# Sixteen of 64 rank pairs instead of sixteen of 256 in a product-key retrieval

## The chip, the cores and the metric

The kernel runs on one core of a Trainium2 chip, in one launch. The metric is the device time of that launch in microseconds (us). The engines are named as the profile names them: PE is TensorE (matmuls; PEld its weight loads), DVE is VectorE, ACT is ScalarE, POOL is GpSimd, and SP only issues DMAs here. Each engine takes its instructions from its own queue in order, and waits at the head of that queue for what the instruction needs.

## The reference

Two transformer blocks over 512 tokens of width 1024. The change concerns the feed-forward part of the first, a PEER layer: 16384 experts of one neuron each, found by product keys. For each token and each of 8 heads, two halves of a query are scored against 128 keys each, and the best 16 of each half are kept; the 256 sums of a first and a second score are searched for the best 16.

```
s_top, i_top = lax.top_k(s, PEER_TOPK)                     # (tokens, heads, 2, 16)
cand_s = (s_top[:, :, 0, :, None] + s_top[:, :, 1, None, :]).reshape(..., 256)
cand_i = (i_top[:, :, 0, :, None] * PEER_N_KEYS + i_top[:, :, 1, None, :]).reshape(..., 256)
best_s, best_pos = lax.top_k(cand_s, PEER_TOPK)
experts = jnp.take_along_axis(cand_i, best_pos, axis=-1)
g = jax.nn.softmax(best_s, axis=-1)
act = jax.nn.gelu(jnp.einsum('thkd,td->thk', expert_u[experts], xb))
return jnp.einsum('thk,thkd->td', g * act, expert_v[experts])
```

Since both lists of 16 are sorted, a pair of ranks (a, b), counted from 0, has at least (a+1)(b+1)-1 pairs before it, so that it can be among the first 16 only where (a+1)(b+1) is at most 16.

## The kernel before, in words

Every float32 matmul is done as three in a rounded float32 format: a weight tile `raw` of 128 x 1024 is loaded by SP (`weight`, line 857), ACT writes its rounded part `hi` (line 861), DVE the rest `lo = raw - hi` (line 863), and PE multiplies hi by the input's two parts and lo by the first (`mm3`, lines 867 to 869). `hi` and `lo` have three buffers each.

The PEER layer treats its 512 tokens in two ways. The fourth tile of 128 tokens gathers its experts' rows from memory (`gather`, line 164: per step an indirect DMA on POOL, a product with a sum on DVE, line 172, and an accumulation on DVE, line 169). The other 384 tokens are multiplied densely with all experts: 128 products of a weight tile `uT` with 384 tokens (`hidden`, line 372: 24 matmuls of 128 x 384 to a bank `ps_mm`, then a gelu on ACT). A product is called p0, p1, ... here in the order in which PE takes them. A dense matrix of gates, zero where an expert was not chosen, is built from one-hot matrices (`build`, line 182: `oh` and `gi` on DVE, `ps_S` on PE) and multiplied in before the second dense product (`output`, line 420).

The stages in order are: queries and first searches (lines 278 to 296, 16 times, over 128 scores each); retrieval beside the first products (lines 388 to 394); build beside further products (lines 400 to 406); the remaining products, each beside the output of the one before; and the outputs of those products that were kept in memory (`spill`).

`retrieve(n)` (line 298) is called for the four token tiles, n = 3 first. I call its four passes retrieval blocks. In each, for 8 heads, POOL adds the 256 sums (`cand`, line 306) and DVE searches them (`top16`, line 270: MAX8, MATCH_REPLACE8, MAX8, FIND_INDEX8 twice, the last three kinds preceded by a short load of the eight values). The places found, 0 to 255, are split in a first and a second rank by a shift and a mask (lines 315 and 317), and each rank is turned to a key index: DVE compares it with 0 to 15 (`eq`, line 321, 128 x 2048), POOL multiplies the 16 one-hot planes with the indices `tif` (line 323), and DVE adds the planes up by halves (lines 329 and 331). A softmax follows (lines 335 to 341), and for three of the tiles a transposition on PE (line 349).

What sets the order: the program interleaves the parts by credits (`Work.go`, line 211). A `yield 1.9` says that a step is worth 1.9 us; after each product, retrieval may use RH = 2.4 us of credit (line 391). From these, the number of products before the second stage follows, and from it the number of products kept in memory, which is rounded up to a multiple of IG = 8 (line 401). The framework's scheduler then gives every engine's queue its final order, by its own estimate of when an instruction's inputs are there.

Of the kernel before, what the change touches and what calls it, by code (L numbers as in the profile page):

```python
# [8 lines left out]
F32 = mybir.dt.float32  # L9
F32R = mybir.dt.float32r  # L10
BF16 = mybir.dt.bfloat16
I32 = mybir.dt.int32
U32 = mybir.dt.uint32
AF = mybir.ActivationFunctionType
ALU = mybir.AluOpType
# [3 lines left out]
P = 128  # L19
# [9 lines left out]
TOPK = 16  # L29
# [102 lines left out]
DT = 3  # L132
AB, LA = 3, 1
NR, TC, IG = 32, 24, 8
RH, GH0, BH, GH1, GF, GO, VP = 2.4, 1.0, 2.3, 1.2, 3.4, 4, 999


def peer(ctx, tc, I, banks, mod, mid, x1, R, vec, gain, ident, weight, mm3, proj, proj_many, split, enter):

    nc = tc.nc  # L140
    T = DT * P
    with ExitStack() as c2:
# [82 lines left out]
        with ExitStack() as c3:  # L225
# [3 lines left out]
            h = (hh, hl)  # L229
# [7 lines left out]
            with tc.tile_pool(name="tn", bufs=1) as tn:  # L237
# [6 lines left out]
                for c in HALVES:  # L244
                    for k in range(KB):
# [4 lines left out]
                                                       op0=ALU.add, op1=ALU.subtract)  # L250
# [6 lines left out]
            pq = c4.enter_context(tc.tile_pool(name="pq", bufs=1))  # L257
            tq = c4.enter_context(tc.tile_pool(name="tq", bufs=2))
# [2 lines left out]
            nc.vector.tensor_copy(iob, iof)  # L261
            ioa = pq.tile([P, TOPK, P], BF16, name="ioa")
            nc.vector.tensor_copy(ioa, iof[:, 0:TOPK, 0:1].broadcast_to([P, TOPK, P]))
            keysT = pq.tile([P, NHP, P], F32, name="keysT")
            nc.sync.dma_start(keysT, I["keysT"])

# [31 lines left out]
            def retrieve(n):  # L298
# [2 lines left out]
                tv = top[:, n].rearrange("p (h j) k -> p h j k", j=2)  # L301
                bs = tq.tile([P, 8, TOPK], F32, tag="bs", name="bs", bufs=1)
                bx = tq.tile([P, 8, TOPK], U32, tag="bx", name="bx", bufs=1)
                for hd in range(8):
                    cand = tq.tile([P, TOPK, TOPK], F32, tag="cand", name="cand", bufs=2)
                    nc.gpsimd.tensor_tensor(cand, tv[:, hd, 0, :].unsqueeze(2).broadcast_to([P, TOPK, TOPK]),
                                            tv[:, hd, 1, :].unsqueeze(1).broadcast_to([P, TOPK, TOPK]), ALU.add)
                    top16(cand.rearrange("p a b -> p (a b)"), bs[:, hd, :], bx[:, hd, :], 256)
                    yield 1.9
                ij = []  # L310
                for j in range(2):
                    pi = tq.tile([P, P], U32, tag="pi", name="pi", bufs=2)
                    flat = bx.rearrange("p h k -> p (h k)")
                    if j == 0:
                        nc.vector.tensor_scalar(pi, flat, 4, None, op0=ALU.logical_shift_right)
                    else:
                        nc.vector.tensor_scalar(pi, flat, 15, None, op0=ALU.bitwise_and)
                    pf = tq.tile([P, P], BF16, tag="pf", name="pf", bufs=2)
                    nc.vector.tensor_copy(pf, pi)
                    eq = tq.tile([P, TOPK, P], BF16, tag="eq", name="eq", bufs=2)  # L320
                    nc.vector.tensor_tensor(eq, pf.unsqueeze(1).broadcast_to([P, TOPK, P]), ioa, ALU.is_equal)
                    e4 = eq.rearrange("p a (h k) -> p h a k", h=8)
                    nc.gpsimd.tensor_tensor(e4, e4, tif[:, :, j, :].unsqueeze(3).broadcast_to([P, 8, TOPK, TOPK]), ALU.mult)
                    ij.append(eq)
                    yield 1.5
                for j in range(2):
                    eq = ij[j]
                    for w_ in (8, 4, 2):
                        nc.vector.tensor_add(eq[:, 0:w_], eq[:, 0:w_], eq[:, w_:2 * w_])
                    r = tq.tile([P, P], F32, tag="ij%d" % j, name="ij", bufs=1)  # L330
                    nc.vector.tensor_add(r, eq[:, 0], eq[:, 1])
                    ij[j] = r
                    yield 1.5
                ex = tq.tile([P, 8, TOPK], F32, tag="ex", name="ex", bufs=1)
# [978 lines left out]
```

## Time and profile before

| what | us |
|---|---|
| median of three runs (2555.66 to 2558.7) | 2557.21 |
| the profiled execution, its own time | 2557.7 |
| its span, first to last instruction | 2555.9 |
| PE busy in the span | 2476.8 |
| DVE busy in the span | 1787.7 |
| POOL busy in the span | 309.1 |

Busy time is the sum of an engine's instructions in the span; a matmul overlaps with its neighbours, so PE counts as busy also where its clock is low. The profile has the clock that was granted to TensorE beside each stretch: 1.00 is 2.4 GHz, 0.50 is 1.2 GHz. Its mean over this execution is 0.989. A view of waits says for each engine which instruction waited, for whom and how long; a timeline lists single instructions, and a bracket at a row's end says how long the engine had been idle before it, and for what.

### The profile page before, as it was taken

The page shows a single profiled execution, that of the slowest core. Times are in us where ns is not written, and L with a number is a line of the kernel's source. Part 1 is how long each engine was busy: PE and PEld are TensorE (multiplying, and loading weights), DVE is VectorE, ACT ScalarE, POOL GpSimd, SP SyncE. Part 2 cuts the span into 40 slices and gives each one's busy share as a digit, 9 for nine tenths or more (in the row PEclk, how much of TensorE's full clock was granted, in tenths as well). Part 3 has the DMA queues.
Part 4 walks back from the last instruction along what each step waited for, and adds up shares of the span by engine and source line. Part 5 has one row for each costly group of instructions (what it writes and reads, how often), then busy time and mean ns, then how long its engine had stood idle before and what let it go on. Part 6 is the DMA issues. An engine that isn't in the chain of part 4 may idle for free.

```text
span 2555.9 us, 34576 instructions
## 1 busy us (share of the span) xinstructions
PE 2476.8 (97%) x13153; PEld 2135.9 (84%) x13153; DVE 1787.7 (70%) x2977; ACT 1065.5 (42%) x1846; POOL 309.1 (12%) x200
## 2 busy tenths in 40 slices
PE   7899999999899999999999999999999999999998
PEld 4788888888789999999988888886788888888887
DVE  6656745899989888878888888876854334533345
ACT  6524553433344444444444344344533323422343
POOL 0001100004331111123222222210000000000000
PEclk9999999999899999999999999999999999999999
DMA  6343433224667888799998899972112222222254
GB/s 240 128 173 128 159 106 118 103 83 169 218 245 277 300 294 295 288 347 332 339 344 322 310 358 361 359 292 99 58 50 83 91 101 97 94 96 99 101 182 162
DMA packets 145814, 511.28 MB, mean 200 GB/s; under 512 B 13680, under 2 KB 39408, under 8 KB 125936
## 3 DMA queue, kind: packets, MB, share of 16 engines
q1 hardware_dynamic: 114464, 330.14, 36.9%
q0 software_dynamic: 18432, 134.23, 14.1%
q10 hardware_dynamic: 12752, 44.70, 4.6%
q8 instruction: 103, 1.69, 0.3%
q14 instruction: 63, 0.52, 0.1%
HBM read 465.50 MB, written 43.52 MB: 199 GB/s over the span
## 4 chain that ended last, share of the span: by engine, by line
PE 84%; DVE 11%; issue 2%; ACT 2%; DMA 1%; POOL 0%; DVEq 0%; SPq 0%; ACTq 0%; POOLq 0%
PE ps_mm L867 13%; PE ps_mm L868 12%; PE ps_mm L869 12%; PE ps_o L869 7%; PE ps_o L868 7%; PE ps_o L867 7%; PE ps_S L867 3%; PE ps_S L868 3%; PE ps_S L869 3%; PE ps_S L197 3%; DVE lo L863 2%; PE ps_A L869 1%; PE ps_A L868 1%; PE ps_A L867 1%; PE ps_h L867 1%
## 5 line engine op out<-in xcount | busy, mean ns | idle before, releaser
L863 DVE TENSOR_TENSOR lo<-raw,hi 128x1024 fp32r<-128x1024 f32 x473 | 584.1, 1236 | 372.5 <-ACT hi L861 361.0
L861 ACT ACTIVATE hi<-raw 128x1024 fp32r<-128x1024 f32 x474 | 499.8, 1056 | 755.0 <-PE ps_mm L868 424.6
L869 PE MATMUL ps_mm<-hh,lo 128*128 128x512 f32 (+2 forms) x1784 | 654.5, 367 | 27.2 <-DVE lo L863 27.0
L867 PE MATMUL ps_mm<-hh,hi 128*128 128x512 f32 (+2 forms) x1784 | 661.4, 372 | 7.5 <-ACT gv L1065 2.4
L868 PE MATMUL ps_mm<-hl,hi 128*128 128x512 f32 (+2 forms) x1784 | 655.3, 367 | 2.4 <-DVE hl L926 2.2
L869 PEld LDWEIGHTS ps_mm<-hh,lo 128*128 128x128 f32 x1784 | 339.8, 190 | 65.3 <-DVE lo L863 30.2
L867 PEld LDWEIGHTS ps_mm<-hh,hi 128*128 128x128 f32 x1784 | 339.1, 191 | 45.5 <-ACT gv L1065 2.9
L868 PEld LDWEIGHTS ps_mm<-hl,hi 128*128 128x128 f32 x1784 | 340.1, 191 | 39.1 <-DVE hl L926 3.3
L178 POOL DMA_INDIRECT rows<-in_uv,dix x128 | 217.9, 1702 | 748.2 <-DVE act L427 190.0
L867 PE MATMUL ps_o<-hi,wh 128*128 128x512 f32 x768 | 298.9, 389 | 1.4 <-ACT wh L925 1.4
L869 PE MATMUL ps_o<-hi,wl 128*128 128x512 f32 x768 | 299.7, 390 | 0.6 <-DVE wl L926 0.5
L868 PE MATMUL ps_o<-lo,wh 128*128 128x512 f32 x768 | 299.2, 390 | 0.0
L172 DVE SCALAR_TENSOR_TENSOR rows<-rows,hn 128x1024 f32<-128x1024 f32 x128 | 159.9, 1250 | 18.6 <-ACT act L377 8.3
L869 PEld LDWEIGHTS ps_o<-hi,wl 128*128 128x128 f32 x768 | 144.1, 188 | 31.9 <-DVE wl L926 2.1
L169 DVE SCALAR_TENSOR_TENSOR accn<-rows,wgt,accn 128x1024 f32<-128x1024 f32 x128 | 167.2, 1306 | 4.4 <-ACT wgt L175 2.9
L867 PEld LDWEIGHTS ps_o<-hi,wh 128*128 128x128 f32 x768 | 144.2, 188 | 31.1 <-ACT wh L925 1.7
L868 PEld LDWEIGHTS ps_o<-lo,wh 128*128 128x128 f32 x768 | 144.1, 188 | 29.6
L925 ACT ACTIVATE wh<-act 128x384 fp32r<-128x384 f32 x104 | 54.7, 526 | 240.2 <-PE ps_o L868 219.1
L193 DVE TENSOR_TENSOR gi<-oh,gt 128x1536 bf16<-128x1536 bf16 x96 | 91.3, 954 | 0.9
L191 DVE TENSOR_TENSOR oh<-iob,ji 128x1024 bf16<-128x1024 bf16 x96 | 65.8, 688 | 26.8 <-PE ps_S L197 26.2
L197 PE MATMUL ps_S<-gi,oh 128*128 128x128 bf16 x1152 | 78.1, 219 | 0.0
L868 PE MATMUL ps_S<-hl,hi 128*128 128x512 f32 x200 | 78.0, 390 | 0.0
(398 smaller groups left out, 3589.2 us busy)
## 6 DMA issues: line engine op xcount, KB each, us to landing
raw<-in_uT SPq DMA_DIRECT2D x128, 512.0 KB
raw<-in_uv SPq DMA_DIRECT2D x128, 512.0 KB
raw<-in_win SPq DMA_DIRECT2D x82, 512.0 KB
raw<-in_wd SPq DMA_DIRECT2D x44, 512.0 KB
act<-act ACTq DMA_DIRECT2D x52, 384.0 KB
act<-act SPq DMA_DIRECT2D x52, 384.0 KB
gs<-stage ACTq DMA_DIRECT2D x16, 1152.0 KB
ring<-gs SPq DMA_DIRECT2D x12, 1536.0 KB
```

The source lines that it names most:

```text
L169: nc.vector.scalar_tensor_tensor(accn, rows.pop(k - 3)[:, D:], wgt[:, c], accn, op0=ALU.mult, op1=ALU.add)
L172: paced(nc.vector.scalar_tensor_tensor(r[:, :D], r[:, :D], 1.0, hn, op0=ALU.mult, op1=ALU.mult, accum_out=dot[:, c]))
L178: paced(nc.gpsimd.indirect_dma_start(out=r, out_offset=None, in_=I["uv"], in_offset=bass.IndirectOffsetOnAxis(ap=dix[:, k:k + 1], axis=0)))
L191: nc.vector.tensor_tensor(oh, io, each(ji[:, t0 // 4], 2), ALU.is_equal)
L193: nc.vector.tensor_tensor(gi, oh[:, 1].unsqueeze(1).broadcast_to([P, 3, 2, P, 2]), each(gt[:, t0 // 4], 3), ALU.mult)
L197: nc.tensor.matmul(g_ps[:, t, :], oh[:, 0, t // 2, :, t % 2], gi[:, j, t // 2, :, t % 2], start=j == 0, stop=j == 2)
L861: nc.scalar.activation(hi, raw, AF.Copy)
L863: (nc.gpsimd if pool else nc.vector).tensor_sub(lo, raw, hi.bitcast(F32))
L867: nc.tensor.matmul(ps, w[0], x[0], start=first, stop=False)
L868: nc.tensor.matmul(ps, w[0], x[1], start=False, stop=False)
L869: nc.tensor.matmul(ps, w[1], x[0], start=False, stop=last)
L925: nc.scalar.activation(hi, src, AF.Copy)
```

## The change

The searched table is 64 wide instead of 256. First rank 0 is paired with second ranks 0 to 15, first ranks 1 to 3 with 0 to 7, first ranks 4 to 7 with 0 to 3, and first ranks 8 to 15 with 0 alone: 16 + 24 + 16 + 8 = 64 places, which contain all pairs that can be among the first 16. POOL writes the table for all 8 heads at once in four instructions, into one buffer. A place is no longer split by shift and mask. The first rank is the number of row starts that the place has passed: DVE compares the place with the 16 starts (`ios`, `is_ge`), POOL multiplies with the differences of neighbouring indices (`td`), and the sum of the planes is the index. The second rank is the place under a mask of 15, 7, 3 or 0 (`low`), which POOL works out from the place (`cf`, three `step` instructions, two additions, `low`), and DVE applies (`pi`). The planes are added by neighbours instead of by halves. A search step's credit falls from 1.9 to 1.3.

```diff
--- before.py
+++ after.py
@@ -132,6 +132,7 @@
 DT = 3
 AB, LA = 3, 1
 NR, TC, IG = 32, 24, 8
+NC = 64
 RH, GH0, BH, GH1, GF, GO, VP = 2.4, 1.0, 2.3, 1.2, 3.4, 4, 999
 
 
@@ -261,6 +262,11 @@
             nc.vector.tensor_copy(iob, iof)
             ioa = pq.tile([P, TOPK, P], BF16, name="ioa")
             nc.vector.tensor_copy(ioa, iof[:, 0:TOPK, 0:1].broadcast_to([P, TOPK, P]))
+
+            widths = [16] + [8] * 3 + [4] * 4 + [1] * 8
+            ios = pq.tile([P, TOPK, P], BF16, name="ios")
+            for a in range(TOPK):
+                nc.gpsimd.memset(ios[:, a], float(sum(widths[:a])))
             keysT = pq.tile([P, NHP, P], F32, name="keysT")
             nc.sync.dma_start(keysT, I["keysT"])
 
@@ -301,34 +307,54 @@
                 tv = top[:, n].rearrange("p (h j) k -> p h j k", j=2)
                 bs = tq.tile([P, 8, TOPK], F32, tag="bs", name="bs", bufs=1)
                 bx = tq.tile([P, 8, TOPK], U32, tag="bx", name="bx", bufs=1)
+                cand = tq.tile([P, 8, NC], F32, tag="cand", name="cand", bufs=1)
+                for a0, na, nb in ((0, 1, 16), (1, 3, 8), (4, 4, 4), (8, 8, 1)):
+                    c0 = sum(widths[:a0])
+                    shape = [P, 8, na, nb]
+                    nc.gpsimd.tensor_tensor(cand[:, :, c0:c0 + na * nb].rearrange("p h (a b) -> p h a b", b=nb),
+                                            tv[:, :, 0, a0:a0 + na].unsqueeze(3).broadcast_to(shape),
+                                            tv[:, :, 1, 0:nb].unsqueeze(2).broadcast_to(shape), ALU.add)
+                td = tq.tile([P, 8, TOPK], F32, tag="td", name="td", bufs=1)
+                nc.gpsimd.tensor_copy(td[:, :, 0:1], tif[:, :, 0, 0:1])
+                nc.gpsimd.tensor_tensor(td[:, :, 1:], tif[:, :, 0, 1:], tif[:, :, 0, :TOPK - 1], ALU.subtract)
                 for hd in range(8):
-                    cand = tq.tile([P, TOPK, TOPK], F32, tag="cand", name="cand", bufs=2)
-                    nc.gpsimd.tensor_tensor(cand, tv[:, hd, 0, :].unsqueeze(2).broadcast_to([P, TOPK, TOPK]),
-                                            tv[:, hd, 1, :].unsqueeze(1).broadcast_to([P, TOPK, TOPK]), ALU.add)
-                    top16(cand.rearrange("p a b -> p (a b)"), bs[:, hd, :], bx[:, hd, :], 256)
-                    yield 1.9
+                    top16(cand[:, hd], bs[:, hd, :], bx[:, hd, :], NC)
+                    yield 1.3
                 ij = []
+
+                flat = bx.rearrange("p h k -> p (h k)")
+                cf = tq.tile([P, P], F32, tag="cf", name="cf", bufs=1)
+                nc.gpsimd.tensor_copy(cf, flat)
+                steps = []
+                for at, drop in ((16, -8.0), (40, -4.0), (56, -3.0)):
+                    st_ = tq.tile([P, P], F32, tag="st%d" % at, name="step", bufs=1)
+                    nc.gpsimd.tensor_scalar(st_, cf, float(at), drop, op0=ALU.is_ge, op1=ALU.mult)
+                    steps.append(st_)
+                nc.gpsimd.tensor_tensor(steps[0], steps[0], steps[1], ALU.add)
+                nc.gpsimd.tensor_tensor(steps[0], steps[0], steps[2], ALU.add)
+                low = tq.tile([P, P], U32, tag="low", name="low", bufs=1)
+                nc.gpsimd.tensor_scalar(low, steps[0], 15.0, None, op0=ALU.add)
                 for j in range(2):
-                    pi = tq.tile([P, P], U32, tag="pi", name="pi", bufs=2)
-                    flat = bx.rearrange("p h k -> p (h k)")
-                    if j == 0:
-                        nc.vector.tensor_scalar(pi, flat, 4, None, op0=ALU.logical_shift_right)
-                    else:
-                        nc.vector.tensor_scalar(pi, flat, 15, None, op0=ALU.bitwise_and)
+                    if j:
+                        pi = tq.tile([P, P], U32, tag="pi", name="pi", bufs=1)
+                        nc.vector.tensor_tensor(pi, flat, low, ALU.bitwise_and)
                     pf = tq.tile([P, P], BF16, tag="pf", name="pf", bufs=2)
-                    nc.vector.tensor_copy(pf, pi)
+                    nc.vector.tensor_copy(pf, pi if j else flat)
                     eq = tq.tile([P, TOPK, P], BF16, tag="eq", name="eq", bufs=2)
-                    nc.vector.tensor_tensor(eq, pf.unsqueeze(1).broadcast_to([P, TOPK, P]), ioa, ALU.is_equal)
+                    nc.vector.tensor_tensor(eq, pf.unsqueeze(1).broadcast_to([P, TOPK, P]), ioa if j else ios,
+                                            ALU.is_equal if j else ALU.is_ge)
                     e4 = eq.rearrange("p a (h k) -> p h a k", h=8)
-                    nc.gpsimd.tensor_tensor(e4, e4, tif[:, :, j, :].unsqueeze(3).broadcast_to([P, 8, TOPK, TOPK]), ALU.mult)
+                    by = tif[:, :, 1, :] if j else td
+                    nc.gpsimd.tensor_tensor(e4, e4, by.unsqueeze(3).broadcast_to([P, 8, TOPK, TOPK]), ALU.mult)
                     ij.append(eq)
                     yield 1.5
                 for j in range(2):
+
                     eq = ij[j]
-                    for w_ in (8, 4, 2):
-                        nc.vector.tensor_add(eq[:, 0:w_], eq[:, 0:w_], eq[:, w_:2 * w_])
+                    for w_ in (1, 2, 4):
+                        nc.vector.tensor_add(eq[:, 0::2 * w_], eq[:, 0::2 * w_], eq[:, w_::2 * w_])
                     r = tq.tile([P, P], F32, tag="ij%d" % j, name="ij", bufs=1)
-                    nc.vector.tensor_add(r, eq[:, 0], eq[:, 1])
+                    nc.vector.tensor_add(r, eq[:, 0], eq[:, 8])
                     ij[j] = r
                     yield 1.5
                 ex = tq.tile([P, 8, TOPK], F32, tag="ex", name="ex", bufs=1)
```

With the credits, the four blocks now take 4 x (8 x 1.3 + 7.5) / 2.4 = 30 products instead of 4 x (8 x 1.9 + 7.5) / 2.4 = 38, and 96 products instead of 104 are kept in memory.

The scheduler moves instructions of all engines in this stage. Three places are shown. Line numbers are those of each kernel's own file: line 863 before is line 889 after, 272 to 276 are 278 to 282, and 323 is 348.

First, DVE's queue in the first retrieval block, in the midst of the searches. Before:

```order
L863 TENSOR_TENSOR lo<-raw,hi 128x1024 [waits DMAHW1_49,PE_49,Activation_49]
L272 MAX bs<-cand 128x8 [waits Pool_49]
L863 TENSOR_TENSOR lo<-raw,hi 128x1024 [waits DMAHW2_49,PE_49,Activation_49]
L273 MATCH_REPLACE rest<-bs,cand 128x256 [waits DVE_49]
L275 MAX_INDEX bx<-bs,cand 128x8
L274 MAX bs<-rest 128x8 [waits DVE_49]
L272 MAX bs<-cand 128x8 [waits Pool_49]
L276 MAX_INDEX bx<-bs,rest 128x8 [waits DVE_49]
L273 MATCH_REPLACE rest<-bs,cand 128x256 [waits DVE_49]
L275 MAX_INDEX bx<-bs,cand 128x8
L274 MAX bs<-rest 128x8 [waits DVE_49]
L863 TENSOR_TENSOR lo<-raw,hi 128x1024 [waits DMAHW4_49,PE_49,Activation_49]
```

After:

```order
L889 TENSOR_TENSOR lo<-raw,hi 128x1024 [waits DMAHW7_49,PE_49,Activation_49]
L278 MAX bs<-cand 128x8 x2
L279 MATCH_REPLACE rest<-bs,cand 128x64 [waits DVE_49]
L281 MAX_INDEX bx<-bs,cand 128x8
L280 MAX bs<-rest 128x8 [waits DVE_49]
L279 MATCH_REPLACE rest<-bs,cand 128x64
L282 MAX_INDEX bx<-bs,rest 128x8 [waits DVE_49]
L280 MAX bs<-rest 128x8 [waits DVE_49]
L281 MAX_INDEX bx<-bs,cand 128x8
L282 MAX_INDEX bx<-bs,rest 128x8 [waits DVE_49]
L889 TENSOR_TENSOR lo<-raw,hi 128x1024 [waits DMAHW0_49,PE_49,Activation_49]
```

The searches of two whole heads now stand between two `lo`. Counted over the queue, from one cast of `tif` to the next (the fourth block: to the first `oh`), the retrieval blocks hold 7, 6, 10 and 16 `lo` before, and 4, 4, 4 and 18 after. The gather's instructions of lines 172 and 169 stand in them 0, 0, 8 and 14 times before, and 0, 0, 1 and 15 times after.

Second, DVE's queue at the end of the first block, from the second ranks to the first sum of planes. Before, up to the next `lo`:

```order
L315 TENSOR_SCALAR pi<-bx 128x128 [waits DVE_49]
L317 TENSOR_SCALAR pi<-bx 128x128
L319 CAST pf<-pi 128x128 [waits DVE_49] x2
L321 TENSOR_TENSOR eq<-pf,ioa 128x2048 [waits DVE_49] x2
L338 TENSOR_REDUCE sm<-ex 128x8 [waits Activation_49]
L272 MAX bs<-cand 128x8 [waits Pool_49]
L339 RECIPROCAL sm<-sm 128x8 [waits DVE_49]
L273 MATCH_REPLACE rest<-bs,cand 128x256 [waits DVE_49]
L329 TENSOR_TENSOR eq<-eq 128x1024 [waits Pool_49]
L341 TENSOR_TENSOR gate<-ex,sm 128x128 [waits DVE_49]
L863 TENSOR_TENSOR lo<-raw,hi 128x1024 [waits DMAHW5_49,PE_49,Activation_49]
```

After (the next `lo` stands five rows further down):

```order
L344 TENSOR_TENSOR eq<-pf,ios 128x2048 [waits DVE_49]
L340 TENSOR_TENSOR pi<-bx,low 128x128 [waits Pool_49]
L278 MAX bs<-cand 128x8 [waits DVE_49]
L342 CAST pf<-pi 128x128 [waits DVE_49]
L279 MATCH_REPLACE rest<-bs,cand 128x64 [waits DVE_49]
L344 TENSOR_TENSOR eq<-pf,ioa 128x2048 [waits DVE_49]
L364 TENSOR_REDUCE sm<-ex 128x8 [waits Activation_49]
L280 MAX bs<-rest 128x8 [waits DVE_49]
L355 TENSOR_TENSOR eq<-eq 128x8x128 [waits Pool_49]
```

The second comparison now comes behind a wait for POOL (`pi<-bx,low`), while the first `eq` is ready for POOL before it.

Third, POOL's queue after the searches of the first block, with the next block's table between the steps. After:

```order
L327 CAST cf<-bx 128x128 [waits DVE_49]
L314 TENSOR_TENSOR cand<-top 128x8x16
L331 TENSOR_SCALAR step<-cf 128x128 [waits Pool_49]
L331 TENSOR_SCALAR step<-cf 128x128 x2
L333 TENSOR_TENSOR step<-step 128x128 [waits Pool_49]
L314 TENSOR_TENSOR cand<-top 128x8x8
L334 TENSOR_TENSOR step<-step 128x128 [waits Pool_49]
L336 TENSOR_SCALAR low<-step 128x128 [waits Pool_49]
L348 TENSOR_TENSOR eq<-eq,td 128x8x16x16 [waits DVE_49]
L348 TENSOR_TENSOR eq<-eq,tif 128x8x16x16 [waits DVE_49]
```

Before, nothing but the `cand` of the next heads stands ahead of the two multiplications (line 323). Nine instructions, from `cf` to `low`, stand there now.

## Rows read from the trace of the kernel before

**Rows 1.** The page: PE's share of the span; engines on the chain that ended last.
```profile
PE 2476.8 (97%) x13153; PEld 2135.9 (84%) x13153; DVE 1787.7 (70%) x2977; ACT 1065.5 (42%) x1846; POOL 309.1 (12%) x200
...
PE 84%; DVE 11%; issue 2%; ACT 2%; DMA 1%; POOL 0%; DVEq 0%; SPq 0%; ACTq 0%; POOLq 0%
```

**Rows 2.** Waits of PE, 575 to 745: us in total, times, longest.
```profile
PE ps_mm L869 <- DVE lo L863: 24.3, 5, 9.2
```

**Rows 3.** Stretches: length, busy PE PEld DVE ACT POOL, clock, DMA share, GB/s.
```profile
575.00:745.00 170.00, 145.48 (x782) 143.04 (x782) 167.06 (x382) 62.17 (x102) 72.54 (x49) 0.92 0.54 195
745.00:1100.00 355.00, 354.99 (x2787) 344.59 (x2787) 305.33 (x368) 170.24 (x402) 57.30 (x33) 1.00 0.81 293
1100.00:1305.00 205.00, 203.15 (x1035) 185.51 (x1035) 164.47 (x198) 88.64 (x168) 58.20 (x36) 1.00 0.92 338
```

**Rows 4.** Timeline of PE: start, length, instruction, idle before it.
```profile
570.13 0.33 PE L869 MATMUL ps_mm<-hh,lo 128*128 128x384 f32 x1
...
574.29 0.33 PE L869 MATMUL ps_mm<-hh,lo 128*128 128x384 f32 x1
...
579.66 0.33 PE L867 MATMUL ps_mm<-hh,hi 128*128 128x384 f32 x1
...
606.67 0.69 PE L869 MATMUL ps_mm<-hh,lo 128*128 128x384 f32 x1 [5.62 <-DVE lo L863]
...
739.06 0.69 PE L869 MATMUL ps_mm<-hh,lo 128*128 128x384 f32 x1 [6.31 <-DVE lo L863]
```

**Rows 5.** Stretches of 2 us around the third stall, columns as in rows 3.
```profile
690.00:692.00 2.00, 0.09 (x1) 0.09 (x1) 2.00 (x4) 0.00 (x0) 1.25 (x1) 0.50 0.00 0
...
694.00:696.00 2.00, 2.00 (x8) 2.00 (x8) 2.00 (x10) 0.00 (x0) 0.00 (x0) 0.50 0.98 399
...
698.00:700.00 2.00, 2.00 (x14) 2.00 (x13) 2.00 (x6) 1.00 (x3) 0.19 (x1) 1.00 0.61 188
```

**Rows 6.** Timeline of POOL in the first retrieval block, columns as in rows 4.
```profile
584.67 0.62 POOL L306 TENSOR_TENSOR cand<-top 128x256 f32<-128x256 f32 x1 [3.07 <-DVE bx L275]
586.51 0.62 POOL L306 TENSOR_TENSOR cand<-top 128x256 f32<-128x256 f32 x1 [1.22 <-DVE bx L275]
...
596.51 8.22 POOL L323 TENSOR_TENSOR eq<-eq,tif 128x2048 bf16<-128x2048 bf16 x2 [3.44 <-DVE eq L321]
```

**Rows 7.** Timeline of DVE beside those two multiplications.
```profile
597.68 0.41 DVE L272 MAX8 bs<-cand 128x8 f32<-128x256 f32 x1
...
601.15 4.13 DVE L329 TENSOR_TENSOR eq<-eq 128x1024 bf16<-128x1024 bf16 x1 [2.53 <-POOL eq L323]
...
605.40 1.21 DVE L863 TENSOR_TENSOR lo<-raw,hi 128x1024 fp32r<-128x1024 f32 x1
606.54 1.55 DVE L329 TENSOR_TENSOR eq<-eq 128x512 bf16<-128x512 bf16 x4
```

**Rows 8.** Timeline of DVE in the first searches, over 128 scores.
```profile
478.12 0.47 DVE L272 MAX8 top<-sv 128x8 f32<-128x128 f32 x2
...
480.45 0.47 DVE L272 MAX8 top<-sv 128x8 f32<-128x128 f32 x2
```

**Rows 9.** One line's instructions: the casts of `tif`, lengths and first and last start.
```profile
L300 DVE CAST tif<-tix x4: 279/284/289, 574.2 to 695.3; 128x256 f32<-128x256 uint32 x4
```

**Rows 10.** Timeline of DVE at the last of the stalls.
```profile
737.79 2.35 DVE L863 TENSOR_TENSOR lo<-raw,hi 128x1024 fp32r<-128x1024 f32 x2
```

**Rows 11.** The page: the gather's two instructions on DVE, busy, mean ns.
```profile
L172 DVE SCALAR_TENSOR_TENSOR rows<-rows,hn 128x1024 f32<-128x1024 f32 x128 | 159.9, 1250 | 18.6 <-ACT act L377 8.3
...
L169 DVE SCALAR_TENSOR_TENSOR accn<-rows,wgt,accn 128x1024 f32<-128x1024 f32 x128 | 167.2, 1306 | 4.4 <-ACT wgt L175 2.9
```

**Rows 12.** POOL by line: the nearest one-input instruction of 128 x 128.
```profile
masks.py:199 POOL TENSOR_SCALAR_AFFINE_SELECT ident<-ident 128x128 f32<-128x128 f32 x1 | 0.3, 287 | 0.0
```

**Rows 13.** Timeline of PE from the last transposition to the first build.
```profile
761.34 0.27 PE L349 MATMUL ps_T<-ident,gg 128*128 128x128 f32 x1
...
770.10 0.85 PE L197 MATMUL ps_S<-gi,oh 128*128 128x128 bf16 x12
```

## The prediction

> **What bounds the kernel now.** I read the page first. PE is busy for 97% of the span, and 84% of the chain that ended last is PE [rows 1]. PE's work is the same in both kernels, so a change outside PE can only move the time where PE waits or runs slowly. The stretches of the stages show where that is. While the retrieval runs (575 to 745), PE is busy for 145.5 of 170 us at a mean clock of 0.92, and DVE for 167.1; in the build and the stage after it PE is busy for practically the whole length at a clock of 1.00 [rows 3]. PE's waits in that stretch are all of one kind: it waits for a `lo` of DVE, five times, 24.3 us in sum and 9.2 at the longest [rows 2]. The timeline of PE puts four of the five at one place of the program each: the first ends at 606.67 after 5.62 us, the last at 739.06 after 6.31 [rows 4].
>
> POOL's timeline tells what that place is. From 596.51 its two multiplications of one-hot planes last 8.22 us [rows 6]. DVE's MAX8 runs beside them at its usual 0.41 us, but a sum of two tensors that was free to start at 601.15, when the first was over, lasts 4.13 us, to the end of the second [rows 7]. So a DVE instruction with two tensors to read waits out a whole POOL instruction. `lo` is such an instruction, it stands behind the sums in DVE's queue, and PE runs dry once in each block. A stall has a second price: around the third one the clock is 0.50 still at 694 to 696, where PE does 8 matmuls in 2 us instead of 14 [rows 5].
>
> **How much is lost now.** A product takes 4.16 us on PE, from a matmul at 570.13 to the 24th after it at 574.29; p3 begins at 579.66 [rows 4], and needs its `lo` at its third matmul, 0.35 us later, at 580.0. Without loss p33 would need its own thirty products later, at 704.8. It got it at 739.06. So 34.3 us are lost, and that is all that this change can give back. How much it will give back depends on when DVE gets through its queue.
>
> **DVE's time before, from the first `tif` at 574.2 [rows 9] to the `lo` of p33, which ends at 738.9 (first of two in 2.35 us from 737.79 [rows 10]): 164.7 us.** Its parts: a head's search over 256 takes 1.84 us (POOL's tables, released by the searches, start 584.67 and 586.51 [rows 6]); of 32 heads, two had their first MAX8 and FIND_INDEX8 done earlier, four instructions of about 0.37 (0.41 [rows 7] less the overlap), so 32 x 1.84 - 1.5 = 57.4. 31 `lo` at 1.14 (605.40 to 606.54 [rows 7]): 35.3. Fifteen instructions of the gather stand in the queue up to there, at 1.2 (means of 1.25 and 1.31, less the overlap of neighbours [rows 11]): 18.0. The rest, 54.0, is what follows the searches in four blocks, 13.5 each: comparisons, sums, softmax, and the two multiplications that hold DVE up.
>
> **DVE's time after.** By the order, the comparable place (the first `lo` behind the multiplications of the fourth block) is the `lo` of p19, the 17th from the first `tif`, since the blocks hold 4 `lo` each and the fourth has 5 up to there.
> - Searches over 64: no row has them. Over 128 two heads take 2.33 us (478.12 to 480.45 [rows 8]), 1.17 each, so 64 places cost 0.335 and a head over 64 should take 0.83: 26.7 us. Bounds: 1.17 if nothing falls below 128, and a quarter of 1.84, 0.46, in proportion. I take the line through the two rows.
> - 17 `lo`: 19.4. Five instructions of the gather up to there: 6.0.
> - What follows the searches: same comparisons, sums by size, and multiplications; a shift, a mask and their casts become one mask and two casts. 54.0 again.
> - New: DVE's `pi` waits for POOL's chain from `cf` to `low`, nine instructions. The nearest rows are 0.62 for 256 elements of two tensors [rows 6], so 0.33 for 128, and 0.287 for one input [rows 12]. Nine at 0.33 are 3.0 us a block, and the little that DVE has ready beside them reads two tensors and queues with them; I take 2.75, 11.0 in four blocks. Bounds: nothing (all of it beside DVE's comparison and `lo`), and nine times 0.62, 22.3. Behind the wait on DVE's queue stand the searches of the next block and the next `lo`, for which PE waits.
>
> The Trainium skill, "GPSIMD Engine Reference", section "Engine selection", would rather have such steps on VectorE: two-input operations are about twice as slow on GpSimd, one-input ones run at line rate there. Its section "Elementwise — side-by-side cycle accounting" has 2.6 cycles per element for two inputs. An estimate by that page: 0.28 us for each of four two-input steps of 128 and 0.11 for each of five others, 1.7 us a block, and the sum would be 5 us lower. No row here shows a POOL instruction of that kind at 128 elements alone.
>
> Together 26.7 + 19.4 + 6.0 + 54.0 + 11.0 = 117.1 us, so that the `lo` of p19 comes at 691.3. PE needs it sixteen products after 580.0, at 646.6. The loss is 44.7 us, 10.4 more than now. Put otherwise: DVE is through 47.6 us earlier, but PE has been given 14 products fewer, 58.2 us of its work. The searches' relief went into bringing the retrieval forward.
>
> Later: the 8 products less in this stage are done in the later stages at PE's full pace [rows 3], and 14 `lo` behind p18 stand with nothing but the gather between them, so no new stall is due there. From the last transposition to the first build matmul 8.8 us pass [rows 13]; the order has one product and half of one in between where it had two, so up to 2.3 us could show. I take 0.6, since DVE is ahead there. The new writes of `ios` come in the first searches, where POOL is idle; a `lo` could wait out one of them, 0.3 at most by the nearest row [rows 12]. The rest of the queues differ only by the eight products.
>
> Sum: 2557.7 of the profiled execution + 10.4 + 0.6 = 2568.7; that execution was 0.5 above the median, so 2568 for the median.
>
> **Rivals.**
> - *The relief reaches PE.* If `lo` ran two products ahead when POOL's 7.2 us of multiplication begin, as DVE's shorter searches would allow, no stall would remain: 34 us less, 2523; with half of it, 2540. For it speaks that DVE is the bound now [rows 3]. Against it speaks the order, 4 `lo` a block: 4 x 4.16 = 16.6 us of PE's work against a block of DVE of some 27 us. It decides from about 0.55 us a head with a hidden POOL chain.
> - *Nothing to see.* With both uncertain prices halfway to their lower ends (0.65 a head, 1.4 us a chain), 11.4 us go from the sum and the loss is as now: 2557.
> - *Slower still.* A search that costs over 64 what it costs over 128 adds 32 x 0.34 = 10.7: 2579. The place is the same, and the point is the fixed part of the five instructions.
> - *It doesn't do what it says*: the table is a quarter, but POOL's two multiplications, which make the stalls, stay as they are, 8.2 us a block; then only their number and not their length could change, which is the forecast's own ground, 2568.
>
> **Chances and range.** Forecast (slower by 5 to 16 us) 0.50; slower still 0.22; nothing to see 0.13; the relief reaches PE, wholly or in part, 0.15. A measurement of this kernel can tell 0.2%, 5 us, from no change. So slower 0.72, same 0.13, faster 0.15. The unknown prices reach from 12 + 11 us below to 11 + 11 + 2 above the sum, 2545 to 2592; the ends together are unlikely, and I take 2546 to 2584.
>
> **What would show it.** Right: the four stalls are still there, each ending with a `lo` behind POOL's second multiplication, now at about p6, p10, p14 and p19; DVE is busy or held throughout the first three blocks; a POOL row of 0.3 us for each step; a head's search over 64 places of about 0.83 us. Wrong: PE's waits for `lo` sum to under 20 us; or the multiplications fall where PE has two products in hand; or a stall outside of this stage.

## The result, and the profile after

Before 2558.1 us (median of 6 runs, 2555.7 to 2561.1), after 2573.1 (6 runs, 2571.3 to 2575.2): a ratio of 1.0058, 95% interval 1.0045 to 1.0071. The change makes the kernel slower by 15.0 us, where the forecast was 2568, slower by 11. The profiled execution after spans 2571.9 us, 16.0 more than before's.

The page after, as in [rows 1]:

```profile
PE 2479.3 (96%) x13153; PEld 2137.8 (83%) x13153; DVE 1758.8 (68%) x2973; ACT 1068.6 (42%) x1846; POOL 317.0 (12%) x236
...
PE 87%; DVE 8%; ACT 2%; issue 1%; POOL 1%; DMA 1%; SPq 0%; DVEq 0%; ACTq 0%; POOLq 0%
```

DVE has less to do (1758.8 us for 1787.7) and PE the same 13153 matmuls, yet the time is longer. PE's waits from 575 to 745, as in [rows 2], and the same three stretches as in [rows 3], show where:

```profile
PE ps_mm L895 <- DVE lo L889: 40.6, 7, 12.3
```

```profile
575.00:745.00 170.00, 129.37 (x687) 126.83 (x687) 134.29 (x391) 57.40 (x94) 76.74 (x66) 0.87 0.50 175
745.00:1100.00 355.00, 355.00 (x2789) 344.68 (x2788) 303.78 (x362) 171.78 (x401) 57.71 (x33) 1.00 0.84 296
1100.00:1305.00 205.00, 205.00 (x1034) 185.65 (x1033) 170.06 (x208) 89.58 (x172) 62.77 (x38) 1.00 0.93 340
```

PE waits for `lo` 16.3 us more, all in the retrieval stage; behind it PE is busy throughout, at full clock, as before. PE's timeline, as in [rows 4]: the start of p3, and the ends of the four long waits, at p6, p10, p14 and p19; three shorter ones, 3.1 us together, stand at p11 to p13.

```profile
581.06 0.33 PE L893 MATMUL ps_mm<-hh,hi 128*128 128x384 f32 x1
...
604.36 0.69 PE L895 MATMUL ps_mm<-hh,lo 128*128 128x384 f32 x1 [10.30 <-DVE lo L889]
...
629.33 0.69 PE L895 MATMUL ps_mm<-hh,lo 128*128 128x384 f32 x1 [5.30 <-DVE lo L889]
...
662.09 0.69 PE L895 MATMUL ps_mm<-hh,lo 128*128 128x384 f32 x1 [9.54 <-DVE lo L889]
...
697.36 0.69 PE L895 MATMUL ps_mm<-hh,lo 128*128 128x384 f32 x1 [12.33 <-DVE lo L889]
```

By the prediction's reckoning p3 needs its `lo` at 581.4 and p19, sixteen products on, at 648.0. It came at 697.4: 49.4 us are lost, for 34.3 before, 15.1 more. Of the other 0.9 of the 16.0 us, 1.4 lie ahead of the stage (p3 starts 1.4 later than in [rows 4]; in four runs below that change nothing ahead of it, it starts between 579.7 and 584.6) and -0.5 behind it.

One block of it, the first, on DVE (start, length, instruction, idle before it) and on POOL:

```profile
575.82 0.35 DVE L278 MAX8 bs<-cand 128x8 f32<-128x64 f32 x2
...
577.51 0.33 DVE L278 MAX8 bs<-cand 128x8 f32<-128x64 f32 x2
...
584.82 1.21 DVE L889 TENSOR_TENSOR lo<-raw,hi 128x1024 fp32r<-128x1024 f32 x1
...
586.28 1.22 DVE L344 TENSOR_TENSOR eq<-pf,ios 128x2048 bf16<-128x2048 bf16 x1
592.79 0.29 DVE L340 TENSOR_TENSOR pi<-bx,low 128x128 uint32<-128x128 uint32 x1 [5.30 <-POOL low L336]
593.00 0.22 DVE L278 MAX8 bs<-cand 128x8 f32<-128x64 f32 x1
593.14 3.55 DVE L342 CAST pf<-pi 128x128 bf16<-128x128 uint32 x1
...
598.14 0.21 DVE L280 MAX8 bs<-rest 128x8 f32<-128x64 f32 x1
598.27 4.03 DVE L355 TENSOR_TENSOR eq<-eq 128x1024 bf16<-128x1024 bf16 x1
...
603.09 1.21 DVE L889 TENSOR_TENSOR lo<-raw,hi 128x1024 fp32r<-128x1024 f32 x1
```

```profile
584.85 2.92 POOL L314 TENSOR_TENSOR cand<-top 128x128 f32<-128x128 f32 x1 [8.34 <-DVE bx L281]
...
588.20 0.28 POOL L327 CAST cf<-bx 128x128 f32<-128x128 uint32 x1
588.45 0.41 POOL L314 TENSOR_TENSOR cand<-top 128x128 f32<-128x128 f32 x1
588.92 2.09 POOL L331 TENSOR_SCALAR step<-cf 128x128 f32<-128x128 f32 x3
590.98 0.46 POOL L333 TENSOR_TENSOR step<-step 128x128 f32<-128x128 f32 x1
...
592.21 0.55 POOL L336 TENSOR_SCALAR low<-step 128x128 uint32<-128x128 f32 x1
592.84 3.77 POOL L348 TENSOR_TENSOR eq<-eq,td 128x2048 bf16<-128x2048 bf16 x1
598.10 3.66 POOL L348 TENSOR_TENSOR eq<-eq,tif 128x2048 bf16<-128x2048 bf16 x1 [1.49 <-DVE eq L344]
```

Two heads are searched in 1.69 us. Then DVE stands for 5.30 us, since `pi` waits for `low`; from 593 to 602 it is held twice by POOL's multiplications (an instruction of DVE is called held here when it lasts until an instruction of POOL has ended), first a cast, then a sum; and the `lo` for which PE waits comes behind that. All waits of DVE for `low` from 575 to 700:

```profile
DVE pi L340 <- POOL low L336: 17.0, 4, 5.3
```

### The profile page after: what moved, and what is told of

Read it like the earlier page. It is cut to its first block, busy times and chain, and to the rows that moved or that the text cites. A ratio compares the mean times of both kernels' runs of the same rounds, so it can differ in the third digit from the quotient of the medians.

```text
span 2571.9 us, 34544 instructions
## 1 busy us (share of the span) xinstructions
PE 2479.3 (96%) x13153; PEld 2137.8 (83%) x13153; DVE 1758.8 (68%) x2973; ACT 1068.6 (42%) x1846; POOL 317.0 (12%) x236
## 3 DMA queue, kind: packets, MB, share of 16 engines
q8 instruction: 103, 1.69, 0.3%
## 4 chain that ended last, share of the span: by engine, by line
PE 87%; DVE 8%; ACT 2%; issue 1%; POOL 1%; DMA 1%; SPq 0%; DVEq 0%; ACTq 0%; POOLq 0%
PE ps_mm L893 13%; PE ps_mm L895 13%; PE ps_mm L894 13%; PE ps_o L895 7%; PE ps_o L894 7%; PE ps_o L893 7%; PE ps_S L894 3%; PE ps_S L893 3%; PE ps_S L895 3%; PE ps_S L198 3%; PE ps_h L893 2%; PE ps_h L895 2%; PE ps_h L894 2%; PE ps_A L894 1%; PE ps_A L895 1%; PE ps_A L893 1%
## 5 line engine op out<-in xcount | busy, mean ns | idle before, releaser
L895 PE MATMUL ps_mm<-hh,lo 128*128 128x512 f32 (+2 forms) x1720 | 634.0, 369 | 43.7 <-DVE lo L889 43.7
L893 PE MATMUL ps_mm<-hh,hi 128*128 128x512 f32 (+2 forms) x1720 | 640.4, 374 | 6.2 <-ACT gv L1091 2.5
L894 PE MATMUL ps_mm<-hl,hi 128*128 128x512 f32 (+2 forms) x1720 | 634.8, 369 | 2.0 <-DVE hl L952 1.7
L895 PEld LDWEIGHTS ps_mm<-hh,lo 128*128 128x128 f32 x1720 | 328.5, 191 | 81.8 <-DVE lo L889 46.9
L893 PEld LDWEIGHTS ps_mm<-hh,hi 128*128 128x128 f32 x1720 | 327.2, 191 | 43.8 <-ACT gv L1091 2.9
L894 PEld LDWEIGHTS ps_mm<-hl,hi 128*128 128x128 f32 x1720 | 328.4, 191 | 39.3 <-DVE hl L952 3.2
L893 PE MATMUL ps_h<-hh,hi 128*128 128x384 f32 x256 | 85.9, 336 | 0.0
L895 PE MATMUL ps_h<-hh,lo 128*128 128x384 f32 x256 | 85.8, 336 | 0.0
```

The costliest lines, as they stand in the source:

```text
L893: nc.tensor.matmul(ps, w[0], x[0], start=first, stop=False)
L894: nc.tensor.matmul(ps, w[0], x[1], start=False, stop=False)
L895: nc.tensor.matmul(ps, w[1], x[0], start=False, stop=last)
```

## The experiments

Each was timed beside the kernel before in the same session (2557.2 to 2558.6 us there); the ratio is to that. "After" is the changed kernel, 1.0058. The scheduler orders the queues anew for each, so the number of `lo` in the four blocks, 4, 4, 4 and 18 in after, is given where it is another, counted from the trace from one `tif` to the next.

**POOL's chain on DVE.** From `cf` to `low` it has seven instructions, as the trace above shows; the section on the change, the prediction and the expectations say nine, since I had counted the two of `td`, which stay on POOL. The edit, shown for `cf` and the same for all seven:

```diff
-                nc.gpsimd.tensor_copy(cf, flat)
+                nc.vector.tensor_copy(cf, flat)
```

> The changed kernel with its nine small instructions from cf to low on DVE instead of POOL; all else as it is. My theory (DVE's queue reaches the lo behind each pair of multiplications too late, and the waits for POOL's chain, 17.0 us in four blocks, are part of that time): the 17.0 go, nine DVE instructions of 0.13 to 0.2 us a block come, some 6.5 in sum, and by the order the last stall moves from p19 to p21, two lo more for DVE (2.3) and two products more for PE (8.3). Loss 49.4 - 17.0 + 6.5 + 2.3 + 1.2 - 8.3 = 34 instead of 49.4: 2558 (2553 to 2564), as the kernel before. PE still stalls behind POOL's multiplications, at p7, p10 and p14, 20 to 32 us in sum. Rival (DVE has other work beside the chain, or waits just as long for something else): the nine instructions come on top, 2579.

Measured 2559.2, 1.0003 (0.9995 to 1.0012). PE's waits for `lo` are 25.6 us, the long ones at p7, p10, p14 and p21, and DVE no longer waits for POOL's `low`. The loss up to p21 is 34.1 us, as expected. So POOL's chain, which the narrow table needs but which is no part of the search, cost 14 us by standing on POOL, nearly the whole 15. Not all of that is the wait: the blocks hold 5, 4, 5 and 16 `lo` here, and by the expectation's own terms 10.5 us are the chain's and 4.8 come with the two `lo` more ahead of the last stall. No run parts the two. DVE is still held by the multiplications, one-input instructions too:

```profile
PE ps_mm L895 <- DVE lo L889: 25.6, 5, 9.6
```

```profile
588.49 3.71 DVE L336 TENSOR_SCALAR low<-step 128x128 uint32<-128x128 f32 x1
```

**The credits.** `yield 1.3` becomes `yield 1.9`.

> The changed kernel with a head's search entered at 1.9 again in the credits instead of 1.3; no instruction is other, 38 products instead of 30 come before the second stage. My theory (what counts is how many lo stand in DVE's queue up to each pair of multiplications): by the order the first three blocks still hold 4 lo each, so the first three stalls stay, some 25 us of waits and 36 us of loss up to p15; only the fourth block gets more lo in front, and its stall of 12.3 us goes or shrinks under 3 us: 2561 (2556 to 2566). Rival one (the number of products in the stage is what the change lost; with them back, DVE is through 43 us earlier than before and PE never dry): 2523 to 2530. Rival two (the number does not matter): 2573.

Measured 2563.1, 1.0016 (1.0007 to 1.0024). The trace is of the slowest execution, 2569.95. The first three waits are still there, 10.0, 6.4 and 9.3 us; the fourth is gone (none over 1.5 behind p14). The blocks hold 5, 3, 4 and 27 `lo`: the eight products help where their `lo` come, in the fourth block, and nowhere else. Both rivals fall. PE's waits from 575 to 745:

```profile
PE ps_mm L895 <- DVE lo L889: 31.4, 9, 10.0
```

**The multiplications on DVE, in after and in before.**

```diff
-                    nc.gpsimd.tensor_tensor(e4, e4, ...
+                    nc.vector.tensor_tensor(e4, e4, ...
```

> The changed kernel with the eight multiplications of one-hot planes on DVE instead of POOL; the nine small instructions stay on POOL. My theory (a two-tensor DVE instruction waits out a whole POOL multiplication, and that puts lo behind): DVE gets eight instructions of about 2.2 us (an estimate from lo, 1.13 for 1024 elements), 17.6 in sum, and loses some 28 us of instructions held for 3.4 to 4.6 us each, and what waits for POOL's result; the order has more lo in each block, since the sums no longer stand together. Waits of PE for lo 10 to 20 us instead of 40.6, none over 6: 2540 (2532 to 2552). Rival (DVE is bound by the amount of its work, not by being held): 17.6 us more, 2590.

> The kernel before, with 256 places, and with its eight multiplications on DVE instead of POOL. My theory: as for the changed kernel, DVE gets 17.6 us and loses the held instructions; no DVE instruction of the retrieval lasts 3 us or more, PE's waits fall from 24.3 to 10 to 18 us, 2543 (2535 to 2552). Rival (DVE is bound by the amount of its work): 17.6 us more, 2576.

Measured 2546.0, 0.9946 (0.9933 to 0.9959), and 2541.7, 0.9938 (0.9925 to 0.9952): 27 and 17 us faster than the kernels they come from, though DVE gets eight multiplications of 2.28 us, 18 us, more. Its busy time on the page even falls, from 1758.8 to 1747.0 and from 1787.7 to 1779.2: time in which DVE was held had counted as busy. Such a multiplication in after's variant, and PE's waits, 40.6 in after:

```profile
592.45 2.28 DVE L348 TENSOR_TENSOR eq<-eq,td 128x2048 bf16<-128x2048 bf16 x1
```

```profile
PE ps_mm L895 <- DVE lo L889: 12.4, 3, 5.0
```

The rival, that the amount of DVE's work counts, called for 17.6 us more in both, and falls. In after's variant DVE still waits 15.7 us for `low`. The order is another one here too, 6, 5, 9 and 10 `lo` in the blocks and, in before's variant, 8, 9, 10 and 11 instead of 7, 6, 10 and 16, so that these runs don't tell how much of the gain is the holds' and how much the order's.

**Each multiplication cut into four, on POOL.**

```diff
-                    nc.gpsimd.tensor_tensor(e4, e4, by...
+                    for h0 in range(0, 8, 2):
+                        h = slice(h0, h0 + 2)
+                        nc.gpsimd.tensor_tensor(e4[:, h], e4[:, h], by[:, h]...
```

> The changed kernel with each of POOL's multiplications cut into four instructions of two heads (128x512 elements each); the same work on POOL, and DVE's queue in the same order but for a sum or two. My theory (a DVE instruction waits out whole POOL instructions, so that the length of one instruction sets the price): no DVE instruction is held for over some 1.2 us where it was 3.4 to 4.7; each block comes to its lo 3 to 5 us earlier, 12 to 20 in sum: 2557 (2550 to 2564). Rival (what counts is when POOL's products are there, since the sums in front of lo need them): POOL needs as long or longer for them, PE's stalls stay at 10, 5, 9.5 and 12 us: 2573.

Measured 2572.8, 1.0063 (1.0049 to 1.0076): nothing gained, my expectation failed. No DVE instruction there lasts over 2.1 us, as expected, but now POOL is held by them in turn, its four pieces take 5.18 us instead of 3.77, and DVE's first sum waits for the product itself. POOL's first multiplication, and then all that DVE waited for from 575 to 700:

```profile
591.46 5.18 POOL L350 TENSOR_TENSOR eq<-eq,td 128x512 bf16<-128x512 bf16 x4
```

```profile
DVE pi L340 <- POOL low L336: 17.0, 4, 5.3
DVE eq L357 <- POOL eq L350: 10.3, 6, 3.0
```

So two waits lay over each other, the hold and the wait for the product. Only the first is seen in after, as a long DVE instruction; with it shortened the second shows, as idle time.

**The order alone.** The first instruction of a head's search, the comparisons and the sums are pinned behind what the program issued before them (shown for the search):

```diff
-                nc.vector.max(v[:, 0:8], vals)
+                ins = nc.vector.max(v[:, 0:8], vals)
+                if n == NC:
+                    tc.keep_in_program_order(ins)
```

> The changed kernel, every instruction as it is and on its engine, but the first DVE instruction of each head's search, the comparisons eq and the sums over planes are pinned behind what the program issued before them. In DVE's queue the blocks now hold 4, 8, 8 and 8 lo up to the second comparison instead of 3, 4, 4 and 4, and a lo stands in front of the first sum in three of four blocks. My theory (the place of lo in DVE's queue sets the loss): by the queue and the durations measured, stalls at p6 (9), p14 (3), p21 (9) and p28 (7), 29 us of waits instead of 40.6, and a loss of 35 to 41 us instead of 49.4: 2560 (2553 to 2565). Rival (the amount of work on DVE and POOL in the stage and their waits for each other set it, in whatever order): 2573.

Measured 2564.2, 1.0024 (1.0014 to 1.0034): 9 us faster than after by order alone, at the slow end of my range. The blocks hold 4, 9, 8 and 9 `lo`. Waits at p6, p13 and p14, p21 and p28 of 8.7, 2.2, 2.9, 10.0 and 9.0 us, and a loss up to p28 of 40.9 us instead of 49.4. DVE still waits 15.7 us for `low` and is held beside each multiplication.

```profile
PE ps_mm L897 <- DVE lo L891: 32.8, 5, 10.0
```

**The order and the cut.**

> As the kernel with the pinned order, with each of POOL's multiplications cut into four. With the order of the scheduler the cut gave nothing, and there the first sum, which needs POOL's product, stood in front of lo. My theory now (two waits lie over each other, that for POOL's port and that for POOL's product, and cutting the instruction helps only a lo that stands in front of the sum): here lo gets in between the pieces, 2 to 3 us earlier in three blocks, 6 us faster than the pinned order alone: 2554. Rival (POOL's multiplications take longer by what DVE does between the pieces, and all comes back at the next wait for POOL): the same time as with the pinned order alone, within 3 us.

Measured 2563.0, 1.0018 (1.0009 to 1.0028), overlapping the one above: 1.2 us, not 6, and within the rival's 3. The `lo` of p6 does get in between the pieces, and PE's first wait falls from 8.7 to 4.8 us:

```profile
599.50 2.07 DVE L893 TENSOR_TENSOR lo<-raw,hi 128x1024 fp32r<-128x1024 f32 x1
601.49 1.54 DVE L359 TENSOR_TENSOR eq<-eq 128x1024 bf16<-128x1024 bf16 x1
606.00 0.29 DVE L308 CAST tif<-tix 128x256 f32<-128x256 uint32 x1 [2.97 <-POOL eq L352]
```

Behind it DVE waits 2.97 us for POOL's second product in front of `tif`. PE's waits for `lo` fall by 9.9 us over the stage, and 5.1 come back as its waits for sums at the transpositions:

```profile
PE ps_mm L899 <- DVE lo L893: 22.9, 4, 7.4
PE ps_T L379 <- DVE ij L361: 5.1, 3, 1.8
```

How much of the remaining difference is real these runs don't tell.

**Both on DVE.** The chain and the multiplications, order by the scheduler.

> The changed kernel with both the nine small instructions and the multiplications on DVE; POOL keeps the sums of candidates, the differences and the gather. By DVE's queue and the durations measured so far (2.21 us a multiplication, some 1.7 us a block for the nine), DVE gets 17.7 + 6.8 us and loses all holds and waits; in the order the blocks have 5 to 8 lo each. PE waits 6 to 14 us in sum, none over 4: loss some 12 us instead of 49.4, 2534 (2526 to 2542). Rival (24.5 us of work more on the engine that bounds the stage outweigh the wait for POOL in the kernel with the multiplications on DVE alone): no better than that one, 2546 or more.

Measured 2532.3, 0.9900 (0.9885 to 0.9915): 41 us faster than after, with 18 us of multiplications and the chain more on DVE's queue (6, 7, 8 and 9 `lo` in the blocks). The two moves add up: the chain's is worth 14 us with the multiplications on POOL and 14 with them on DVE (2546.0 to 2532.3), the multiplications' 27 either way (2559.2 to 2532.3).

**And the indices in bf16.** `tif` and `td` are declared BF16.

> As the kernel with both on DVE, with the key indices tif and their differences td in bf16 instead of float32, which holds them exactly; DVE's order is the same. My theory: a multiplication with all its operands in bf16 takes the 1.13 us of the comparison eq over as many elements instead of 2.21, so DVE has 8.6 us less; PE's waits fall under 5 us, and the stage is bound by PE: 2526 (2520 to 2532). Rival (the broadcast operand, not its type, makes the 2.21): no change, 2534.

Measured 2533.6, 0.9909 (0.9894 to 0.9924), and the multiplication still takes 2.28 us. The rival holds. The comparison `eq`, 1.21 us for as many elements, repeats `pf` over planes, so that neighbours are read in a row; the multiplication repeats each index over 16 neighbours. The operation is another one as well. So the type is excluded as the cause; that it is the way of repeating is argued, not shown. The Trainium skill, "VectorE: DVE Perf Modes", section "Mode 2×_1P — pack two bf16 into one 32-bit read", wants 16-bit types and a step of one; the two durations agree with it.

**And the credits at 1.9.**

> As the kernel with both on DVE in bf16, and a head's search entered at 1.9 in the credits: 38 products before the second stage instead of 30, 104 kept in memory... as in the kernel before. My theory: once DVE keeps ahead, the number of products in the stage is worth nothing: the same 2526 within 4 us. Rival (the products given to the stage still decide, as they did with POOL's multiplications): 5 to 10 us faster than with 30.

Measured 2529.2, 0.9890 (0.9875 to 0.9905), 4.4 us faster than with 30 products: between the two. The blocks hold 6, 6, 8 and 19 `lo`. PE's waits for `lo` up to 745 are 3.7 us, one of them 3.0.

**And the pinned order (indices in float32 again, credits at 1.9).**

> Candidate that should beat both kernels: search over 64 places, the nine small instructions and the multiplications on DVE, the pinned order, and 1.9 in the credits for a head's search (38 products before the second stage). By DVE's queue and the durations measured no wait of PE for lo is over 1.5 us and they sum to 3 us; a loss of 3 us or less instead of 49.4: 2525 (2521 to 2530). Rival (without the pinned order the same work took 2529.2, where 7.3 us of waits were left, 3 of them in this stage; the rest is in other stages, and the order gives nothing more): 2529.

Measured 2524.9, 0.9870 (0.9855 to 0.9885): 33 us faster than the kernel before, 48 faster than after. Against the run above, 4 us come with the pinned order, which has 8, 9, 10 and 12 `lo` in the blocks. PE does not wait for one `lo` in the stage, and DVE has time left; the stretch, columns as in [rows 3]:

```profile
575.00:745.00 170.00, 167.22 (x996) 165.59 (x995) 160.07 (x445) 78.65 (x138) 36.67 (x32) 1.00 0.74 252
```

**The same with 256 places.** Multiplications on DVE, pinned order, credits of before, and before's shift and mask.

> The kernel before, with 256 places and its shift and mask, its multiplications on DVE and the pinned order of the fastest kernel (about as many products, 40 before the second stage). It differs from the fastest kernel by the table of 64 and by the nine small instructions. My theory (with the holds gone the stage is bound by the sum of DVE's work, and now the shorter search counts): DVE has 32 x 1.00 us more for searches and 6.8 less for the nine, some 25 us net; PE stalls at p8, p28 and p38 for 3 to 4 us each, 17 us in sum with the small ones: a loss of 20 to 24 us, 2541 (2535 to 2547). Rival (order and holds were all; the narrow table is worth nothing to PE): 2525 to 2529.

Measured 2544.0, 0.9946 (0.9933 to 0.9960). DVE is busy 168.40 of 170 us there and PE 155.31:

```profile
575.00:745.00 170.00, 155.31 (x868) 150.29 (x866) 168.40 (x400) 69.75 (x114) 36.14 (x42) 0.99 0.64 226
```

So the narrow table, with its chain and its way of adding the planes, is worth 19 us once POOL no longer holds DVE; in the change as it was made, less than nothing. Pinning gives the 256 places nothing (2541.7 without it), but it had little to give: the scheduler's own order has the same 8, 9, 10 and 11 `lo` in the blocks.

## Why the prediction was right, point by point

- *What bounds the stage* was right: DVE's queue up to the `lo` behind each second multiplication. ("Busy or held throughout" it was not: its waits for `low`, 17.0 us, are idle time.) Its place was right too, p6, p10, p14 and p19, and so was the balance, 14 products fewer against a shorter queue. With the same instructions in another order the kernel took 9 us less, with the chain and the multiplications on DVE 41 less.
- *Searches*, 26.7 forecast: 1.69 us for two heads, 0.84 each, 27.3 us in all. The line through 128 and 256 places held.
- *`lo`, gather and the rest*, 19.4 + 6.0 + 54.0 = 79.4 forecast. From DVE's timeline, from `tif` at 575.63 to 697.3, each instruction up to the start of the next: 22.8 + 9.3 + 45.2 = 77.3. The sum was right, the parts were not: the 54.0 was a remainder that held the holds of before, and in after one fell on a `lo` and one on the gather. That eight multiplications would hold DVE about as long as before was in the forecast; on which term they would fall was not.

```profile
657.36 4.67 DVE L889 TENSOR_TENSOR lo<-raw,hi 128x1024 fp32r<-128x1024 f32 x1
...
691.49 4.67 DVE L173 SCALAR_TENSOR_TENSOR rows<-rows,hn 128x1024 f32<-128x1024 f32 x1
```

- *POOL's chain*, 11.0 forecast, 17.0 measured: the term that was too small, and with it the forecast. I priced nine instructions at 0.33 us by rows of another kind. There are seven, and in the first block they take 3.84: 0.28 for `cf`, 2.09 for three steps, 0.46 for each of two sums, 0.55 for `low`; a step takes 0.65 or more, where the sign named was 0.3. Besides, `cf` begins 3.3 us after the last index there (584.9 to 588.2), behind two sums of the next block, the first of which takes 2.92 beside DVE's `lo` and `eq`; in the second block it begins 2.3 us late, in the others at once. The upper bound, 22.3, held. The estimate by the Trainium skill, "GPSIMD Engine Reference", section "Elementwise — side-by-side cycle accounting", 1.7 us a block, is further off. (In the prediction's sum it stands for 4.2 us less, 4 x (2.75 - 1.7), not 5.) The advice of the Trainium skill, "GPSIMD Engine Reference", section "Engine selection", to have such steps on VectorE agrees with the first experiment: 2559.2 instead of 2573.1.
- In sum 121.7 us from `tif` to the `lo` of p19, 117.1 forecast; 4.6 of the 4.7 us by which the loss was forecast too small. The chain's 6.0 too little and 0.6 of the searches stand against 2.1 too much in the second term; that these set off in part is luck. The measured 15.0 lies near the upper end of the 5 to 16 that were given a chance of 0.50.
- *The start of the build*, 0.6: not there. From the last transposition at 745.87 to the first build matmul at 752.25 6.4 us pass, where it was 8.8 in [rows 13].

```profile
745.87 0.27 PE L375 MATMUL ps_T<-ident,gg 128*128 128x128 f32 x1
...
752.25 0.93 PE L198 MATMUL ps_S<-gi,oh 128*128 128x128 bf16 x13
```

- *A DVE instruction with two tensors waits out a POOL instruction* [rows 7]: right, and too narrow. A cast with one input was held for 3.55 us beside a multiplication, a TENSOR_SCALAR for 3.71; MAX8 went through, and beside the cut multiplications a reduction and a reciprocal. The Trainium skill, "SBUF — State Buffer", section "Who interferes with whom", counts casts and tensor_scalar among the forms that can want the port pair shared with GpSimd, and says that whoever comes first holds it for a whole instruction; the traces agree.
- *Rivals.* "The relief reaches PE" was priced right, 2523, and asked for too little: it takes the chain, the multiplications, the order and the credits together (2524.9). "Slower still" got its time half way, not by its mechanism. "Nothing to see" would have needed a cheap chain and searches of 0.65 us; the searches took 0.84, and the kernel with the chain on DVE came out there all the same (1.0003). The fourth had POOL's multiplications unchanged, and they are: 3.77 and 3.66 us in the first block.

The half clock behind a wait [rows 5] is there again. Behind the first wait PE still runs at 0.50, 8 matmuls in 2 us, from 608 to 610, and from the end of that wait to the beginning of the next it takes 19.7 us for four products that take 16.6 at full clock. Behind the second 2.6 us go in this way, behind the third about 2. That is most of what lies between the 40.6 us of waits and the 49.4 lost.

```profile
608.00:610.00 2.00, 2.00 (x8) 2.00 (x8) 2.00 (x21) 0.00 (x0) 0.00 (x0) 0.50 0.66 229
```

## What to carry to other kernels

Here work taken from the engine that bounds a stage was worth what the waited-for instruction gained in its queue against the products taken away; write the queue down up to that instruction, before and after, with the products that the other engine is given meanwhile. A helper engine that hands its result straight back is a wait: with seven small instructions on the busy engine itself the kernel took 14 us less. Where two waits lie over each other, taking away the visible one shows the other.

## What was not expected of the hardware

Holding goes both ways: one of POOL's `cand` sums took 2.92 us beside DVE's `lo` and `eq`, where one of the same size took 0.41 (588.45). A DVE queue heavier by 18 us of multiplications gave a kernel 27 us faster, with POOL's multiplications gone and the order that came with it. A multiplication of 2048 bf16 elements with an operand repeated over neighbours takes 2.28 us with that operand in float32 or bf16; a comparison with one repeated over planes takes 1.21.
